# The output products of the mixing chain, issued in their own step

## The chip, the cores and the metric

The kernel runs on one core of a Trainium2 chip. The metric is device time in microseconds (us), as the median of several runs. Five engines matter here: TensorE (PE: matrix products, with PEld for its weight loads), VectorE (DVE), ScalarE (ACT), GpSimd (POOL) and SyncE (SP, which issues most transfers). Each engine works through its own list of instructions in order and waits on semaphores of the others.

## What is computed

A trunk of two layers over 768 tokens (256 context tokens, 512 latent tokens), width 1024. Each layer mixes tokens in three branches (convolution, differential attention, bidirectional RWKV-7), merges them and adds an MLP. The change is in the RWKV branch, whose core is a recurrence over time for each head and direction:

```
def step(s, inp):
    r_t, w_t, k_t, v_t, kk_t, a_t = inp
    sa = jnp.einsum('bhij,bhj->bhi', s, -kk_t)
    s = (s * w_t[:, :, None, :] + sa[..., None] * (kk_t * a_t)[:, :, None, :]
         + v_t[..., None] * k_t[:, :, None, :])
    return s, jnp.einsum('bhij,bhj->bhi', s, r_t)
```

It runs over 8 heads, forwards and backwards; the two directions' outputs are added.

## The kernel before

The recurrence is worked in chunks of 64 tokens. Two heads make a pair, there are four pairs in a layer, and both directions of a pair go along together. A pair has 12 chunks: two halves of three pieces (`gp` 0 to 5), a piece having two chunks (`q` 0 and 1). For a half, a triangular system is inverted ahead (`half_solve`: products `wps` and `jps`), and then `chain_piece` carries the state X from chunk to chunk. A chunk is a **step** of the chain, 48 in a layer and 96 in all, and has three visits to PE, each of which waits for the one before:

- first products, `ca<-x,ar`: the state against this chunk's rows; then DVE adds (`rhs`);
- second products, `ca<-rhs,j` and `cb<-rhs,j`: the inverse against `rhs`; then ACT and DVE write half of the result each into the tile `gv`;
- third products, `ca<-gv,tok`: the state's update; then DVE adds it to the decayed old state `xp` (made on ACT) and has the new X.

The chunk's outputs are two more kinds of products that are summed in one PSUM tile, `psy` (one buffer for a piece, tag "y", `bufs=1`): `psy<-tr,gv` (four products) and `psy<-ar,x` (four, with the state from before the update; none in a pair's first chunk, where the state is zero). Once a piece's two chunks are in, two instructions copy or add `psy` into the tile `y`: on ACT where `gp` is 0, 2 or 3, on DVE else. Layer 0 needs all outputs, layer 1 only those of latent tokens (`gp` 2 to 5).

Before the change, these products come one step late. A step leaves a note in `self.y_job`; the next step calls `y_products` (line 1264) right behind its own first products, so all eight stand there together, sorted by place, the two kinds in turn. `y_outs` (line 1286) puts the copies behind the next step's `gv` instructions. At the end of a half both are called once more.

PE also has the big products of the whole layer (`mmps`, line 228 like all products, in runs of 128x512 or 128x256), which are independent of the chain for long stretches. What stands in what order is set at build time: `weave` (line 283) keeps a clock for each engine by estimated costs, and takes at each point, of all streams of work (the chain is one, the big products another), the one whose next piece can start first. A stream says with `yield t, engine` when its next piece is ready. A fifth number in the yield, `STICK` (0.2 us), lets the chain go ahead although its input is that much short of ready. The second and third visits had it.

Of the kernel before, what the change touches and what calls it, by code (L numbers as in the profile page):

```python
# [10 lines left out]
F32 = mybir.dt.float32  # L11
F32R = mybir.dt.float32r
I32 = mybir.dt.int32
AF = mybir.ActivationFunctionType
ALU = mybir.AluOpType
# [4 lines left out]
P = 128  # L20
# [33 lines left out]
STICK = 0.2  # L54
# [66 lines left out]
class Trunk:  # L121
# [1139 lines left out]
                self.free("b1", t)  # L1261
        self.x_t = max(self.x_t, t)

    def y_products(self):

        if self.y_job is None:
            return
        st, pi, q, X, first, y = self.y_job
        self.y_job = None
        n, ar, tr, gv = st["n_half"], st["ar"], st["trs"][pi], st["gvs"][pi]  # L1270
        c = 2 * pi + q
        if q == 0:
            self.psy = self.rw.tile([P, 512], F32, tag="y", name="psy", bufs=1)[:, 0:256].rearrange("p (d c t) -> p d c t", d=2, c=2)
        for d in range(2):
            g = 1 - (q ^ d)
            for h in range(2):
                hc = slice(64 * h, 64 * h + 64)
                e = self.product(self.psy[hc, d, q, :], gv[:, 2 * d + q, hc], tr[:, q, g, h, :],
                                 start=True, stop=first, tile_position=(0, 64 * h))
                if not first:  # L1280
                    e = self.product(self.psy[hc, d, q, :], X[:, d, hc], ar[:, d, c, 1, :],
                                     start=False, stop=True, tile_position=(0, 64 * h))
        if q == 1:
            self.y_out = (st, pi, y, e)

    def y_outs(self):

        if self.y_out is None:
            return
        st, pi, y, e = self.y_out  # L1290
        self.y_out = None
        S, V = self.S, self.V
        gp = 3 * st["hh"] + pi
        psy = self.psy
        yield e, "ACT" if gp in (0, 2, 3) else "DVE"
        t0 = [x - self.c0 for x in (128 * gp, 128 * (1 - gp) if gp < 2 else 896 - 128 * gp)]
        for d in range(2):
            src = psy[:, d].rearrange("p c t -> p (c t)")
            if d == 1:
                src = src[:, ::-1]  # L1300
            dst = y[:, t0[d]:t0[d] + 128]
            if gp in (0, 2, 3):
                t = S.activation(out=dst, in_=src, func=AF.Copy)
            else:
                t = V.tensor_tensor(out=dst, in0=src, in1=dst, op=ALU.add)
        st["pp"]["y_t"] = t
        self.pieces[st["n_half"]] = pi

    def chain_piece(self, pi, st, y, need_y):
        pr, S, V = self.pr, self.S, self.V  # L1310
        hh, ar, pc = st["hh"], st["ar"], st["pc"]
        tok, gv, j, tv = st["toks"][pi], st["gvs"][pi], st["j"], st["tvs"][pi]
        gp = 3 * hh + pi
        self.x_t = max(self.x_t, st["tok_t"][pi])
        for q in range(2):
            c = 2 * pi + q
            first = gp == 0 and q == 0
            last = gp == 5 and q == 1
            X = self.xs[self.xi % 2]
            yield self.x_t, "PE"  # L1320
            ga = self.rw.tile([P, 512], F32, tag="ca", name="ca", bufs=1)
            gb = self.rw.tile([P, 512], F32, tag="cb", name="cb", bufs=1)
            gd = [1 - (q ^ d) for d in range(2)]
            gr = [slice(64 * g, 64 * g + 64) for g in gd]
            if first:
                rhs = tv[:, q, :]
            else:
                for d in range(2):
                    e = self.product(ga[gr[d], 0:128], ar[:, d, c, 0, :], X[:, d, :], start=True, stop=True,
                                     tile_position=(0, 64 * gd[d]))  # L1330
                self.y_products()
                if not last:
                    xp = pr.tile([P, 2, 128], F32, tag="xp", name="xp", bufs=1)
                    for d in range(2):
                        S.activation(out=xp[:, d, :], in_=X[:, d, :], func=AF.Copy, scale=pc[:, d, c:c + 1])
                yield e, "DVE"
                rhs = pr.tile([P, 128], F32, tag="rhs", name="rhs", bufs=1)
                t = V.tensor_tensor(out=rhs, in0=ga[:, 0:128], in1=tv[:, q, :], op=ALU.add)
                yield t, "PE", None, None, STICK
            gps = [ga[:, 256:384], gb[:, 0:128]]  # L1340
            for h in range(2):
                hc = slice(64 * h, 64 * h + 64)
                for d in range(2):
                    e = self.product(gps[d][gr[d], hc], j[gr[d], c, h, :], rhs[gr[d], hc], start=True, stop=True,
                                     tile_position=(64 * gd[d], 64 * gd[d]))
            yield e, "DVE"
            t = max(S.activation(out=gv[gr[0], q, :], in_=gps[0][gr[0], :], func=AF.Copy, scale=-1.0),
                    V.tensor_scalar(out=gv[gr[1], 2 + q, :], in0=gps[1][gr[1], :], scalar1=-1.0, scalar2=None, op0=ALU.mult))
            yield from self.y_outs()
            yield t, "PE", None, None, STICK  # L1350
            if not last:
                for d in range(2):
                    for h in range(2):
                        hc = slice(64 * h, 64 * h + 64)
                        e = self.product(ga[hc, 128 + 64 * d:192 + 64 * d], tok[:, d, q, hc], gv[:, 2 * d + q, hc],
                                         start=True, stop=True, tile_position=(0, 64 * h))
                yield e, "DVE"
                Xn = self.xs[(self.xi + 1) % 2]
                for h in range(2):
                    hc = slice(64 * h, 64 * h + 64)  # L1360
                    src = ga[hc, 128:256].rearrange("p (d t) -> p d t", d=2)
                    if first:
                        self.x_t = V.tensor_copy(out=Xn[hc, :, hc], in_=src)
                    else:
                        self.x_t = V.tensor_tensor(out=Xn[hc, :, hc], in0=src, in1=xp[hc, :, hc], op=ALU.add)
                self.xi += 1
            if need_y:
                self.y_job = (st, pi, q, X, first, y)
        if not need_y:
            self.pieces[st["n_half"]] = pi  # L1370
        elif pi == 2:
            yield t, "PE"
            self.y_products()
            yield from self.y_outs()

    def pair_bonus(self, l, p):
        V = self.V
# [100 lines left out]
    def chain(self, l, c0):  # L1478
        for n in range(8):
            p, hh = n // 2, n % 2  # L1480
            pp = self.pairs[p]
            yield 0.0, "DVE", lambda: self.halves[n] is not None and "j_t" in self.halves[n]
            st = self.halves[n]
            st["n_half"] = n
            yield st["j_t"], "DVE"
            yield from self.half_solve(st)
            self.solved = n
            for pi in range(3):
                yield 0.0, "PE", lambda: st.get("n", 0) > pi
                if hh == 0 and pi == 0:  # L1490
                    yield 0.0, "PE", lambda: p < 2 or "out" in self.pairs[p - 2]
                    pp["y"] = self.pe.tile([P, T - c0], F32, tag="y", name="y", bufs=2)
                yield from self.chain_piece(pi, st, pp["y"], 128 * (3 * hh + pi) >= c0)
            if hh == 1:
                self.later.append(lambda p=p: self.pair_out(l, p, c0))

# [31 lines left out]
    def inputs(self, l, full, lat):  # L1528
# [4 lines left out]
        self.halves, self.pieces, self.solved = [None] * 8, [-1] * 8, -1  # L1533
        self.ready, self.stage_t = {}, 0.0
        self.conv_n, self.x_t = 0, 0.0
        self.y_job = self.y_out = None
        self.n_upad = 2
        if len(lat) == 1:
            self.n_upad = 1
# [6 lines left out]
        first = deque({"w": lw, "k": k, "a": la, "r": r, "v": v, "g": lg}[x] for x in UNITS[l])  # L1546
# [697 lines left out]
```

## Time and profile before

| | |
|---|---|
| three runs | 2921.22, 2925.59, 2925.92 us; median 2925.59 |
| the profiled execution | 2913.63 us, of which the span of instructions is 2911.8 us |
| PE / PEld / DVE / ACT / POOL busy | 2768.5 / 2229.7 / 1961.5 / 1299.9 / 104.9 us |
| mean granted TensorE clock | 0.986 |
| the chain's stretch, layer 0 | from 166 to 560 us |
| the chain's stretch, layer 1 | from 1774 to 2213 us |

How to read it: PE is busy in 95% of the span, and the last chain of work runs over PE for 73%. A busy share hides two things, though. A product's row in the trace lasts longer than the distance to the next one, since products overlap, so a short wait can lie within a busy stretch; distances between starts tell more than durations. And each fp32 product of the chain has two rows (the first of the two kinds above: 320 products, 640 rows); the big products have one each.

### The profile page before, as it was taken

What the parts mean: (1) busy time and instruction counts of PE and PEld (TensorE: products, weight loads), DVE (VectorE), ACT (ScalarE), POOL (GpSimd) and SP (SyncE); (2) the same over time, 40 slices, a digit from 0 to 9 for tenths busy, and PEclk for the clock granted to TensorE, in tenths of its full rate; (3) what the DMA queues carried; (4) which work ended last, traced back from release to release, by engine and by line L of the source; (5) the groups of instructions that cost most, each with busy time, mean ns of one, the idle gap of its engine ahead of it and who ended that gap; (6) DMA issues with size and microseconds to landing.
All of it is one profiled execution on the core that took longest, in us unless ns stands there. A gap on an engine that the chain in (4) does not pass through costs nothing.

```text
span 2911.8 us, 56372 instructions
## 1 busy us (share of the span) xinstructions
PE 2768.5 (95%) x22423; PEld 2229.7 (77%) x22423; DVE 1961.5 (67%) x4311; ACT 1299.9 (45%) x2522; POOL 104.9 (4%) x181
## 2 busy tenths in 40 slices
PE   8999999999999999999999999999999888899998
PEld 6777777777788887888888777777777656788887
DVE  6778787489995548764333569889985667644445
ACT  4556655455544224231313356556554653433333
POOL 0000000011000000000000000000000100000000
PEclk9999999999999999999999999999999999999999
DMA  5232223354237633553112223223245535322223
GB/s 210 65 77 70 74 79 90 115 151 127 72 124 271 242 119 120 183 186 101 63 62 69 96 70 86 66 83 83 73 120 155 146 119 160 130 97 96 95 95 104
DMA packets 247751, 330.96 MB, mean 114 GB/s; under 512 B 118256, under 2 KB 124032, under 8 KB 247360
## 3 DMA queue, kind: packets, MB, share of 16 engines
q1 hardware_dynamic: 242160, 311.63, 33.6%
q0 software_dynamic: 3712, 14.17, 2.0%
q8 instruction: 176, 2.88, 0.4%
q10 hardware_dynamic: 1616, 1.56, 0.2%
q14 instruction: 87, 0.71, 0.1%
HBM read 266.32 MB, written 47.60 MB: 108 GB/s over the span
## 4 chain that ended last, share of the span: by engine, by line
PE 73%; DVE 14%; ACT 4%; DMA 3%; issue 2%; SPq 0%; DVEq 0%; POOL 0%; ACTq 0%; POOLq 0%
PE mmps L228 60%; PE ca L228 3%; DVE cacc L92 2%; DVE wl L92 2%; DVE ast L92 2%; PE tps L228 1%; ACT wh L92 1%; PE psy L228 1%; PE jps L228 1%; PE wps L228 1%; PE tvps L228 1%; DVE ap L92 1%; DVE x L92 1%; PE atps L240 1%; PE sps L228 1%
## 5 line engine op out<-in xcount | busy, mean ns | idle before, releaser
L228 PE MATMUL mmps<-hh,wh 128*128 128x512 f32 (+1 forms) x2344 | 850.0, 363 | 22.1 <-DVE k L92 5.7
L228 PE MATMUL mmps<-hh,wl 128*128 128x512 f32 (+1 forms) x2344 | 843.3, 360 | 6.0 <-DVE wl L92 5.9
L228 PE MATMUL mmps<-hl,wh 128*128 128x512 f32 (+1 forms) x2344 | 843.6, 360 | 4.3 <-DVE hl L92 4.1
L92 DVE TENSOR_TENSOR wl<-wr,wh 128x512 fp32r<-128x512 f32 x596 | 412.2, 692 | 473.9 <-ACT wh L92 460.1
L92 ACT ACTIVATE wh<-wr 128x512 fp32r<-128x512 f32 x596 | 375.2, 630 | 707.6 <-PE mmps L228 656.9
L228 PEld LDWEIGHTS mmps<-hh,wh 128*128 128x128 f32 x2344 | 446.9, 191 | 93.4 <-issue 18.1
L228 PEld LDWEIGHTS mmps<-hh,wl 128*128 128x128 f32 x2344 | 446.1, 190 | 77.1 <-DVE wl L92 12.8
L228 PEld LDWEIGHTS mmps<-hl,wh 128*128 128x128 f32 x2344 | 447.3, 191 | 67.5 <-DVE hl L92 7.4
L228 PE MATMUL mmps<-ffl,wh 128*128 128x512 f32 (+1 forms) x792 | 279.3, 353 | 0.0
L228 PE MATMUL mmps<-ffh,wh 128*128 128x512 f32 (+1 forms) x792 | 278.1, 351 | 0.0
L228 PE MATMUL mmps<-ffh,wl 128*128 128x512 f32 (+1 forms) x792 | 277.1, 350 | 0.0
L92 DVE SCALAR_TENSOR_TENSOR cacc<-upad,dww,cacc 128x783 f32<-128x783 f32 (+1 forms) x240 | 215.1, 896 | 4.3
L228 PEld LDWEIGHTS mmps<-ffh,wh 128*128 128x128 f32 x792 | 149.1, 188 | 22.7
L228 PEld LDWEIGHTS mmps<-ffh,wl 128*128 128x128 f32 x792 | 148.9, 188 | 21.5
L228 PEld LDWEIGHTS mmps<-ffl,wh 128*128 128x128 f32 x792 | 149.4, 189 | 20.8
L92 DVE SCALAR_TENSOR_TENSOR x<-mmps,mod,x 128x512 f32<-128x512 f32 (+1 forms) x126 | 80.1, 636 | 46.2 <-PE mmps L228 44.8
L92 POOL TENSOR_TENSOR bk<-bk,pc 128x384 f32<-128x384 f32 x64 | 57.4, 927 | 1200.0 <-PE tps L228 1138.5
L92 DVE SCALAR_TENSOR_TENSOR sq<-mmps,rl 128x512 f32<-128x512 f32 x96 | 56.9, 596 | 40.0 <-ACT rl L92 39.9
L92 ACT ACTIVATE stage<-mmps 128x512 f32<-128x512 f32 (+1 forms) x116 | 59.1, 510 | 51.7 <-PE mmps L228 48.7
L92 ACT ACT_TABLE_LOAD x62 | 79.5, 1283 | 4.2 <-PE mmps L228 2.1
L92 ACT ACTIVATE rl<-mmps 128x512 f32<-128x512 f32 x96 | 49.3, 514 | 67.9 <-PE mmps L228 67.9
L92 DVE TENSOR_REDUCE ast<-sps 128x1 f32<-128x768 f32 (+1 forms) x80 | 67.5, 844 | 17.3 <-PE sps L228 17.3
(317 smaller groups left out, 4377.1 us busy)
## 6 DMA issues: line engine op xcount, KB each, us to landing
wr<-in_w_dram SPq DMA_DIRECT2D x268, 256.0 KB, 2.5
wr<-in_win_dram SPq DMA_DIRECT2D x236, 256.0 KB, 2.7
modw<-in_modw_dram SPq DMA_DIRECT2D x80, 512.0 KB, 4.6
wr<-in_pw_dram SPq DMA_DIRECT2D x48, 256.0 KB, 2.9
wr<-in_wo_dram SPq DMA_DIRECT2D x44, 256.0 KB, 2.6
g<-stage SPq DMA_DIRECT2D x24, 384.0 KB, 3.2
gate<-g SPq DMA_DIRECT2D x24, 384.0 KB, 3.8
scb<-in_modw_dram SPq DMA_DIRECT2D x16, 512.0 KB, 6.5
```

The costliest lines, as they stand in the source:

```text
L92: f(**kw)
L228: self.nc.tensor.matmul(out, lhsT, rhs, **kw)
L240: self.nc.tensor.transpose(out, src, self.ident)
```

## The change

The functions `y_products` and `y_outs` go, with `self.y_job` and `self.y_out`. A local function `outputs` issues the products in their own step: the four `psy<-ar,x` right behind the step's first products, and the four `psy<-tr,gv` right behind the third products, which read the same `gv`. The copies of a piece stand at the piece's end, after its second state update. The chain's first visit gets `STICK` too. The note that a piece is done (`self.pieces`, on which other streams wait) moves into `chain`.

```diff
+        psy = []
+
+        def outputs(pairs, q, end):
+
+            clear = not psy
+            if clear:
+                psy.append(self.rw.tile([P, 512], F32, tag="y", name="psy", bufs=1)[:, 0:256].rearrange("p (d c t) -> p d c t", d=2, c=2))
+            for i, (w, x) in enumerate(pairs):
+                d, h = i // 2, i % 2
+                e = self.product(psy[0][64 * h:64 * h + 64, d, q, :], w, x, start=clear and d == 0, stop=end and q == 1 and d == 1, tile_position=(0, 64 * h))
+            return e
...
-            yield self.x_t, "PE"
+            yield self.x_t, "PE", None, None, STICK
...
-                self.y_products()
+                if need_y:
+                    outputs([(X[:, d, 64 * h:64 * h + 64], ar[:, d, c, 1, :]) for d in range(2) for h in range(2)], q, False)
...
-            yield from self.y_outs()
             yield t, "PE", None, None, STICK
...
+            if need_y:
+                ey = outputs([(gv[:, 2 * d + q, 64 * h:64 * h + 64], tr[:, q, gd[d], h, :]) for d in range(2) for h in range(2)], q, True)
+            if not last:
                 yield e, "DVE"
...
-            if need_y:
-                self.y_job = (st, pi, q, X, first, y)
-        if not need_y:
-            self.pieces[st["n_half"]] = pi
-        elif pi == 2:
-            yield t, "PE"
-            self.y_products()
-            yield from self.y_outs()
+        if need_y:
+            yield ey, "ACT" if gp in (0, 2, 3) else "DVE"
+            t0 = [x - self.c0 for x in (128 * gp, 128 * (1 - gp) if gp < 2 else 896 - 128 * gp)]
+            for d in range(2):
+                src = psy[0][:, d].rearrange("p c t -> p (c t)")
+                if d == 1:
+                    src = src[:, ::-1]
+                dst = y[:, t0[d]:t0[d] + 128]
+                if gp in (0, 2, 3):
+                    t = S.activation(out=dst, in_=src, func=AF.Copy)
+                else:
+                    t = V.tensor_tensor(out=dst, in0=src, in1=dst, op=ALU.add)
+            st["pp"]["y_t"] = t
...
                 yield from self.chain_piece(pi, st, pp["y"], 128 * (3 * hh + pi) >= c0)
+                self.pieces[n] = pi
```

On PE, near the end of layer 1's chain, this is the order before, from the last output products behind a step's first visit to the third visit and on (names as above; `hh`, `hl` and `wh`, `wl` are the high and low parts of inputs and weights):

```order
L228 MATMUL psy<-tr,gv 64x64
L228 MATMUL psy<-ar,x_18086 64x64
L228 MATMUL psy<-tr,gv 64x64
L228 MATMUL psy<-ar,x_18086 64x64
L228 MATMUL ca<-rhs,j 64x64
L228 MATMUL cb<-rhs,j 64x64
L228 MATMUL ca<-rhs,j 64x64
L228 MATMUL cb<-rhs,j 64x64
L228 MATMUL mmps<-hh_17325,wh 128x512
L228 MATMUL mmps<-hl_17326,wh 128x512
L228 MATMUL ca<-gv,tok 64x64 x4
L228 MATMUL mmps<-hh_17325,wl 128x512
```

Now, in the same place, from the first visit on:

```order
L228 MATMUL ca<-x_18086,ar 64x128 x2
L228 MATMUL psy<-ar,x_18086 64x64 x4
L228 MATMUL mmps<-hl_17326,wh 128x512
L228 MATMUL ca<-rhs,j 64x64
L228 MATMUL cb<-rhs,j 64x64
L228 MATMUL ca<-rhs,j 64x64
L228 MATMUL cb<-rhs,j 64x64
L228 MATMUL mmps<-hh_17325,wl 128x512
L228 MATMUL mmps<-hh_17311,wh 128x512
L228 MATMUL ca<-gv,tok 64x64 x4
L228 MATMUL psy<-tr,gv 64x64 x4
L228 MATMUL mmps<-hl_17312,wh 128x512
```

Half of the output products have moved from between the first and second visits to behind the third, and a big product stands between the first two visits.

On DVE, at the last change from one piece to the next in layer 1 (`x` is the new state, `rhs` the next step's sum, `y` the copies of the old piece), the order before:

```order
L92 TENSOR_TENSOR x_18087<-ca,xp 64x2x64 x2
L92 TENSOR_TENSOR rhs<-ca,tv 128x128
L92 TENSOR_SCALAR gv<-cb 64x128
L92 TENSOR_TENSOR y<-psy,y 128x128 x2
L92 TENSOR_TENSOR x_18086<-ca,xp 64x2x64 x2
```

And now:

```order
L92 TENSOR_TENSOR x_18087<-ca,xp 64x2x64 x2
L92 TENSOR_TENSOR y<-psy,y 128x128 x2
L92 TENSOR_TENSOR rhs<-ca,tv 128x128
L92 TENSOR_SCALAR gv<-cb 64x128
L92 TENSOR_TENSOR x_18086<-ca,xp 64x2x64 x2
```

The copies have moved ahead of the next step's `rhs`.

## Rows read from the trace of the kernel before

**Rows 1.** Busy time by stretch: window, length, PE, PEld, DVE, ACT, POOL, clock, DMA.

```profile
166.00:560.00 394.00, 381.53 (x5536) 299.05 (x5534) 288.55 (x861) 221.42 (x505) 22.53 (x36) 1.00 0.29 77
1774.00:2213.00 439.00, 423.30 (x5660) 315.03 (x5659) 381.23 (x1006) 239.08 (x524) 29.26 (x42) 1.00 0.31 84
```

**Rows 2.** PE's waits in layer 0's stretch: total us, times, longest.

```profile
PE wps L228 <- DVE jt L92: 3.5, 5, 1.3
PE ca L228 <- DVE rhs L92: 2.3, 7, 0.6
```

**Rows 3.** PE's waits in layer 1's stretch, same columns.

```profile
PE ca L228 <- DVE rhs L92: 2.1, 6, 0.6
PE ca L228 <- ACT gv L92: 1.4, 3, 0.7
```

**Rows 4.** Timeline, one step in layer 1: start us, duration us, engine, instruction.

```profile
2203.50 0.44 PE L228 MATMUL ca<-x,ar 128*64 128x128 f32 x4
...
2203.77 0.34 PE L228 MATMUL psy<-tr,gv 128*64 128x64 f32 x4
...
2203.99 0.29 DVE L92 TENSOR_TENSOR rhs<-ca,tv 128x128 f32<-128x128 f32 x1
...
2204.39 0.27 PE L228 MATMUL ca<-rhs,j 64*64 64x64 f32 x1
...
2204.77 0.50 PE L228 MATMUL mmps<-hh,wh 128*128 128x512 f32 x1
...
2205.10 0.40 PE L228 MATMUL mmps<-hl,wh 128*128 128x512 f32 x1
...
2205.43 0.45 PE L228 MATMUL ca<-gv,tok 128*64 128x64 f32 x8
...
2205.81 0.50 PE L228 MATMUL mmps<-hh,wl 128*128 128x512 f32 x1
...
2206.00 0.59 DVE L92 TENSOR_TENSOR x<-ca,xp 64x128 f32<-64x128 f32 x2 [0.79 <-PE ca L228]
2206.15 0.39 PE L228 MATMUL mmps<-hh,wh 128*128 128x512 f32 x1
...
2206.38 0.39 PE L228 MATMUL mmps<-hl,wh 128*128 128x512 f32 x1
...
2206.94 0.44 PE L228 MATMUL ca<-x,ar 128*64 128x128 f32 x4
```

**Rows 5.** Timeline of PE in layer 0, a step with four output products alone.

```profile
266.89 0.44 PE L228 MATMUL ca<-x,ar 128*64 128x128 f32 x4
267.16 0.40 PE L228 MATMUL psy<-tr,gv 128*64 128x64 f32 x8
267.49 0.39 PE L228 MATMUL mmps<-hl,wh 128*128 128x256 f32 x1
```

**Rows 6.** Timeline, the copies of a piece, on ACT and on DVE.

```profile
2201.73 0.45 ACT L92 ACTIVATE y<-psy 128x128 f32<-128x128 f32 x2
...
2208.56 0.47 DVE L92 TENSOR_TENSOR y<-psy,y 128x128 f32<-128x128 f32 x2
```

**Rows 7.** Timeline, the last solve of layer 0: products, copies, next products.

```profile
535.40 0.95 PE L228 MATMUL wps<-jt,ta 32*32 32x32 f32 x48
...
536.42 0.56 DVE L92 COPY jt<-wps 32x384 f32<-32x384 f32 x1 [1.36 <-PE wps L228]
...
537.41 0.95 PE L228 MATMUL jps<-j,jt 32*32 32x32 f32 x48
```

**Rows 8.** Tile view of psy: rows, duration min/median/max, first and last start.

```profile
L228 PE MATMUL psy<-tr,gv x640: 219/222/272, 170.3 to 2212.9; 128*64 128x64 f32 x160
L228 PE MATMUL psy<-ar,x x608: 221/222/223, 174.7 to 2213.0; 128*64 128x64 f32 x152
```

**Rows 9.** The page's groups: the loads of ACT's function tables, total and mean ns.

```profile
L92 ACT ACT_TABLE_LOAD x62 | 79.5, 1283 | 4.2 <-PE mmps L228 2.1
```

More of the change, by code (lines that the diff above doesn't have):

```diff
@@ L1262, in half_solve @@
         self.x_t = max(self.x_t, t)
[L1264 to L1306, printed above, removed]
-        self.pieces[st["n_half"]] = pi
     def chain_piece(self, pi, st, y, need_y):
@@ L1311, in chain_piece @@
         hh, ar, pc = st["hh"], st["ar"], st["pc"]
-        tok, gv, j, tv = st["toks"][pi], st["gvs"][pi], st["j"], st["tvs"][pi]
+        tr, tok, gv, j, tv = st["trs"][pi], st["toks"][pi], st["gvs"][pi], st["j"], st["tvs"][pi]
         gp = 3 * hh + pi
+        psy = []
[7 more added lines that the diff above has]
+            return e
         self.x_t = max(self.x_t, st["tok_t"][pi])
@@ L1366, in chain_piece @@
                 self.xi += 1
-            if need_y:
-                self.y_job = (st, pi, q, X, first, y)
-        if not need_y:
-            self.pieces[st["n_half"]] = pi
-        elif pi == 2:
-            yield t, "PE"
-            self.y_products()
-            yield from self.y_outs()
+        if need_y:
[11 more added lines that the diff above has]
+            st["pp"]["y_t"] = t
     def pair_bonus(self, l, p):
@@ L1483, in chain @@
             st = self.halves[n]
-            st["n_half"] = n
             yield st["j_t"], "DVE"
@@ L1535, in inputs @@
         self.conv_n, self.x_t = 0, 0.0
-        self.y_job = self.y_out = None
         self.n_upad = 2
```

## The prediction

> **What bounds the kernel now.** I read the busy time by stretch first. In the two stretches in which the chain runs PE is busy 381.5 of 394 us and 423.3 of 439 us, at full clock [rows 1]; DVE comes next with 381 of 439. So both stretches are as long as PE's work plus PE's waits, about 12.5 and 15.7 us of idle time. The view of waits says what they are: the solve's products waiting for a DVE copy, second visits waiting for `rhs` (2.3 and 2.1 us), third visits waiting for `gv` [rows 2, 3]. Then I read one step in the timeline, to see distances and not durations [rows 4].
>
> The order of both kernels says how far the change reaches. On PE the rows are the same up to the first solve of layer 0, again from the first transpose of the attention to the second layer's solve, and again from the second attention on; each time the attention begins at the same big product (the 1210th and the 6538th width of 512 in both). All products are the same in kind and number. So the big products are the filling of a stretch whose content is fixed: a chain that runs faster ends earlier among them (1139 instead of 1150 in layer 0; 6477 instead of 6472 in layer 1, so there later) and brings the end of the stretch no nearer. What can change is PE's cost of going from one kind of product to another, and its waits.
>
> **The change part by part.**
>
> *A, more alternation.* A big product follows another after 0.23 us (2206.15 to 2206.38). Two of them between the second and third visits take 0.66 us (2204.77 to 2205.43) [rows 4], so an entry of the big products among the small ones costs 0.66 - 0.46 = 0.20 us in all. Counted in the order, the runs of big products (with the normalizing sums) go from 619 to 638. Between first and second visits there are 26 more, since four output products fill half the time that eight did: 41 of 88 such places had only output products in them, none has now. Between third and next first visits there are 20 fewer; the rest are elsewhere. 19 x 0.20 = +3.8 us.
>
> *B, the output products beside their like.* Before: first visit with eight output products 0.27 + 0.62 (2203.50 to 2203.77 to 2204.39), third visit 0.38 (2205.43 to 2205.81) [rows 4]: 1.27 us. The step with four alone shows 0.27 + 0.33 [rows 5]; four behind the third visit, with the same shape, save the 0.10 us that a change of kind costs, so 0.38 - 0.10 + 0.33 = 0.61. After: 0.60 + 0.61 = 1.21. That is -0.06 us; as the 0.62 holds a few hundredths of waiting that belong to C, I take -0.05 for 76 steps (608 rows of `psy<-ar,x`, eight a step [rows 8]) and the same for 16 ends of halves, which had a visit of eight by itself: -4.6 us.
>
> *C, waits for `rhs`.* The first visit starts at 2203.50, `rhs` is done on DVE at 2204.28, the second visit starts at 2204.39: 0.89 us are needed, and first visit and eight products fill just that [rows 4]. With four products and one big one they fill 0.27 + 0.33 + 0.43 = 1.03 (0.43 being 0.23 + 0.20). Of the 4.4 us of idle time before second visits [rows 2, 3] some come from a DVE that is busy elsewhere, and stay: I take half, -2.2 (0 to -4.4).
>
> *D, waits for the new state.* From the third visit to DVE's end of the new state is 2206.59 - 2205.43 = 1.16 us, and with the 0.10 us that `rhs` needed to reach PE, 1.26 [rows 4]. I added up, with distances as above, what the order puts between the third visit and the next first: before, one place of 88 is short of 1.26; now 18 are, as the chain may start 0.2 us early there, by 2.2 us together. +2.2 (0 to +4.4: 18 places at 0.2 us and a margin).
>
> *E, the one buffer for outputs.* A new wait. The next piece's first output products now come one visit after the last piece's; they wait for its copies, and behind them on PE everything waits. The order has 24 such waits, 12 on DVE and 12 on ACT. DVE: copies follow the new state at once and take 0.47 us [rows 6]; the first visit starts 0.10 to 0.35 us after the new state (2206.59 to 2206.94) and its output products 0.27 later, so they stand 0 to 0.2 us. The next `rhs` stands behind the copies on DVE, but starts 0.49 us after the first visit anyway. ACT: the copies can start when the last `psy` product is through, some 0.8 us after the third visit, and take 0.45 [rows 6], so they are done at 1.25, before 1.53 (1.26 + 0.27), unless ACT has something else ahead; in the order it has (an exponential, a split, a copy) in 3 of 12. So 12 x 0.08 + 3 x 0.2 = +1.5, 0.08 and 0.2 being my choice within 0 to 0.2 and 0 to 0.45. The bounds: 0, and 24 full copies, 24 x 0.47 = 11.
>
> *F, the solves and token tiles.* The fills around them change as the mixture moves. Products, copy and next products take 2.0 us from start to start (535.40 to 537.41) [rows 7]; in the new order one solve of layer 0 has only 0.88 us between, and four other places are 0.1 to 0.25 short. +2.0 (-4 to +4: the solves' waits of 3.5 us in layer 0 [rows 2] as the size of what such places move).
>
> *G, ACT.* The order has six more table loads (63 to 69), at 1.28 us [rows 9]: 7.7 us on an engine busy 221 of 394 us [rows 1]. Hidden by its idle time; a few hold back a `gv`. +0.5 (0 to 7.7).
>
> Sum: 3.8 - 4.6 - 2.2 + 2.2 + 1.5 + 2.0 + 0.5 = +3.2 us. On the profiled execution that is 2913.6 + 3.2 = 2916.8; the median of the runs stands 12 us above that execution, and 2925.6 + 3.2 gives **2929**. The runs before differ by 4.7 us, and 0.2% (5.9 us) is about what a measurement of this kernel can tell from no change.
>
> **The rivals.**
>
> *The buffer decides (slower).* Place: the 24 waits of E. Point: copies that end later than 0.27 us after the first visit's start. For it: DVE in layer 1 is 87% busy [rows 1], ACT's queue has whole conversions and table loads of 1.28 us [rows 9], and the planner, which knows nothing of this wait, will not have put anything before it. Against: the chain's rows come first on both engines. At a full copy, +11 instead of +1.5, it gives 2938; slower.
>
> *The drain decides.* The rows show that a product of one kind behind one of another costs about 0.1 us more: 0.33 for four products of which the last is followed by a big one [rows 5], 0.20 for an entry and an exit [rows 4]. If only such changes of kind cost, and the sorting of eight output products into four and four saves nothing, B is zero and the sum 3.2 + 4.6 = +7.8: 2933; slower by 0.27%. For it: the 0.05 us of B are a small difference of rows from two places, one in each layer. Against: the first visits in the two places agree, 0.27 us each [rows 4, 5]. The Trainium skill, TensorEngine Tiling (Array Packing), section Key Properties, says that changing the tiling mode drains TensorE, while changing the tile alone does not. By that rule this rival is right: output products and third products have one mode, and putting them together removes no change of mode. The trace agrees on the cost of an entry (0.20 us) but has no row of the two side by side.
>
> *The waits go (faster).* The chain gets its own way more often (the early start for the first visit, fewer big products between): C in full, -4.4, and none of D to G, as a chain that is ahead has its inputs ready: 3.8 - 4.6 - 4.4 = -5.2, and with the waits for `gv` (1.4 us [rows 3]) and half of the solve's 3.5 [rows 2] gone -8.3: 2917 to 2920. For it: in layer 0 the chain ends 11 widths of big products earlier. Against: in layer 1, where `gv` was waited for, it ends 5 later.
>
> *Nothing moves.* All terms lie within 5 us, and could cancel; this is the forecast's own middle and has no case of its own.
>
> **How the numbers follow.** Forecast (2923 to 2933, mostly within 0.2%) 0.47; the buffer 0.22; the drain 0.12; the waits go 0.19. Faster by over 0.2%: most of the last, and a little for an order that falls well, 0.17. Slower by over 0.2%: buffer and most of the drain, and the upper edge of the forecast, 0.35. Same: 0.48. The range reaches from 2916 (the waits go, in full) to 2940 (the buffer at a full copy and two more), and leaves out what lies beyond both: a solve or an attention that starts late for a reason that the order doesn't show.
>
> **What would show it.** The stretches grow by some 2 us each at the same number of products. B: a third visit and its four output products take 0.61 us from first start to the next kind. C: waits for `rhs` fall to about half of 4.4 us. D: waits for the new state come up, near 2 us. E: a group of waits of `psy` for `y`, on DVE up to 0.2 us each; if they are near 0.5, the buffer decides. A: two big products between visits still take 0.66. The prediction is wrong if the attention no longer starts at the same big product, if the time after 560 and 2213 us changes by more than the runs do, or if one wait of several us appears that no step here names.

## The result, and the profile after

The changed kernel takes 2938.9 us (median of six runs, 2929.2 to 2943.9), the kernel before 2921.5 in the same count of runs: a ratio of 1.0055, 95% interval 1.0034 to 1.0075. It is slower by 17 us, or 0.6%.

The profiled execution of the changed kernel took 2943.9 us, that of the kernel before 2913.6: the first is the slowest of its runs, the second faster than any of the six timed runs before, so the two traces differ by 30 us where the medians differ by 17. I come back to the other 13. First the stretches that answer to [rows 1], same columns; the third number from the end is the granted clock as a share of 2.4 GHz.

```profile
166.00:565.00 399.00, 384.33 (x5534) 297.35 (x5528) 292.19 (x866) 228.92 (x511) 21.40 (x36) 1.00 0.28 74
1786.00:2239.00 453.00, 432.54 (x5664) 322.07 (x5662) 382.09 (x1005) 239.47 (x525) 29.91 (x42) 0.97 0.30 84
```

The stretches are longer by 5 and 14 us; in the second the clock is 0.97 where it was full. For a fair comparison of all kernels I cut the span into five stages that hold the same work everywhere: up to layer 0's first solve; from there to the 2210th big product (width of 512); to layer 1's first solve; to the 7400th big product; the rest. Busy time by stage of the kernel before, second and fourth stage:

```profile
155.40:896.70 741.30, 706.85 (x7561) 564.56 (x7561) 588.00 (x1356) 409.35 (x860) 41.44 (x72) 0.99 0.34 100
...
1780.00:2533.20 753.20, 697.48 (x6871) 522.98 (x6871) 586.24 (x1381) 397.69 (x813) 43.88 (x75) 0.98 0.39 114
```

and all five of the changed kernel:

```profile
0.00:156.30 156.30, 144.30 (x1025) 111.01 (x1025) 106.60 (x309) 78.09 (x147) 11.05 (x23) 0.96 0.42 135
156.30:904.90 748.60, 711.57 (x7561) 563.96 (x7561) 590.37 (x1356) 417.09 (x866) 40.31 (x72) 0.99 0.34 99
904.90:1791.50 886.60, 861.82 (x5298) 736.40 (x5297) 501.50 (x947) 285.16 (x479) 8.58 (x12) 0.99 0.38 128
1791.50:2563.10 771.60, 710.02 (x6871) 531.15 (x6871) 587.48 (x1380) 397.65 (x813) 44.75 (x75) 0.96 0.38 111
2563.10:2941.70 378.60, 363.50 (x1675) 299.64 (x1673) 179.79 (x322) 129.94 (x224) 0.00 (x0) 0.98 0.29 96
```

Stage two grew by 7.3 us, stage four by 18.4. The other three hold the same work in the same order and differ by 0.9, 3.3 and 0.0. PE's waits in the two stretches come next. Before, the groups that stand beside [rows 2, 3] (layer 0, then layer 1):

```profile
PE ca L228 <- DVE x L92: 0.4, 1, 0.4
```

```profile
PE wps L228 <- DVE jt L92: 2.5, 4, 1.0
...
PE jps L228 <- DVE jt L92: 1.9, 5, 0.7
...
PE ca L228 <- DVE x L92: 0.5, 2, 0.4
```

After the change, the groups that answer to them and those that grew (layer 0, then layer 1):

```profile
PE wps L228 <- DVE jt L92: 4.3, 7, 1.4
...
PE ca L228 <- DVE x L92: 1.4, 4, 0.5
...
PE ca L228 <- DVE rhs L92: 0.2, 1, 0.2
```

```profile
PE wps L228 <- DVE jt L92: 5.1, 7, 1.3
PE ca L228 <- DVE rhs L92: 3.6, 8, 1.4
PE jps L228 <- DVE jt L92: 2.2, 7, 0.4
PE ca L228 <- DVE x L92: 2.1, 5, 0.9
```

Waits for `rhs` left layer 0 and came back in layer 1. Waits for the new state (`x`), 0.9 us in three places before, are 3.5 us in nine. The solves wait longest. One ordinary step in the timeline, to set beside [rows 4]:

```profile
2228.25 0.45 PE L228 MATMUL ca<-gv,tok 128*64 128x64 f32 x8
2228.53 0.40 PE L228 MATMUL psy<-tr,gv 128*64 128x64 f32 x8
2228.82 0.59 DVE L92 TENSOR_TENSOR x<-ca,xp 64x128 f32<-64x128 f32 x2 [0.81 <-PE ca L228]
2228.86 0.50 PE L228 MATMUL mmps<-hh,wl 128*128 128x512 f32 x1
2229.20 0.40 PE L228 MATMUL mmps<-hh,wh 128*128 128x512 f32 x1
2229.56 0.44 PE L228 MATMUL ca<-x,ar 128*64 128x128 f32 x4
2229.80 0.43 PE L228 MATMUL psy<-ar,x 128*64 128x64 f32 x8
2230.16 0.50 PE L228 MATMUL mmps<-hl,wh 128*128 128x512 f32 x1
```

Third visit and output products take 0.61 us (2228.25 to 2228.86), first visit and output products 0.60 (2229.56 to 2230.16), both as worked out. From the third visit to the next first visit it is 1.31 us, all of it the way through DVE: the state is written by 2229.41 and PE starts 0.15 later. The last big product started at 2229.20 and gave way after 0.36 us where 0.33 is usual; no row calls that a wait. A big product is recorded as 0.40 long although the next one starts 0.23 after it, so a wait shorter than that difference stands in no list. I therefore also compare start to start: what a run of products of one kind took ahead of a first visit, less what the same run takes at places where nothing is waited for. By that measure the time lost ahead of first visits went from 1.8 to 9.0 us. The size hangs on the pace that is called usual: with the shortest case of the same run in the same trace it goes from 3.6 to 8.0. The Trainium skill, Perfetto Trace Analysis, section Tensor Engine Instruction (MATMUL, LD_WEIGHTS), says that TensorE's reported end is computed from the size of the instruction and not observed; the 0.40 beside a pace of 0.23 fits that.

The longest listed wait for the state is of another kind:

```profile
1898.65 0.45 PE L228 MATMUL ca<-gv,tok 128*64 128x64 f32 x8
...
1899.36 0.53 DVE L92 COPY x<-ca 64x128 f32<-64x128 f32 x2
...
1900.03 0.44 PE L228 MATMUL ca<-x,ar 128*64 128x128 f32 x4 [0.93 <-DVE x L92]
```

DVE is hardly late here: the state is written 1.24 us after the third visit's start, where the ordinary step above takes 1.16. But layer 1 has no output products in this piece, the order has no big product there either, and so PE stands for most of the way through DVE. At other places DVE does come late:

```profile
1981.58 0.45 PE L228 MATMUL ca<-gv,tok 128*64 128x64 f32 x8
...
1982.16 0.56 DVE L92 SCALAR_TENSOR_TENSOR e<-e,e 128x384 f32<-128x384 f32 x1
...
1982.75 0.59 DVE L92 TENSOR_TENSOR x<-ca,xp 64x128 f32<-64x128 f32 x2
...
1983.48 0.44 PE L228 MATMUL ca<-x,ar 128*64 128x128 f32 x4 [0.38 <-DVE x L92]
```

DVE, in the middle of another stream's work, has the state written 1.76 us after the third visit, 0.6 us later than in the ordinary step. What stands between third and first visit covers only a part of that.

### The profile page after: what moved, and what is told of

Its sections match the earlier page's. It is cut to its first block, busy times and chain, and to the rows that moved or that the text cites. A ratio compares the mean times of both kernels' runs of the same rounds, so it can differ in the third digit from the quotient of the medians.

```text
span 2941.7 us, 56384 instructions
## 1 busy us (share of the span) xinstructions
PE 2791.2 (95%) x22423; PEld 2242.2 (76%) x22423; DVE 1965.7 (67%) x4311; ACT 1307.9 (44%) x2528; POOL 104.7 (4%) x181
## 5 line engine op out<-in xcount | busy, mean ns | idle before, releaser
L228 PE MATMUL mmps<-hh,wh 128*128 128x512 f32 (+1 forms) x2344 | 854.9, 365 | 18.8 <-ACT wh L92 5.8
L92 DVE TENSOR_REDUCE ast<-sps 128x1 f32<-128x768 f32 (+1 forms) x80 | 67.5, 844 | 18.3 <-PE sps L228 18.3
```

The source lines that it names most:

```text
L92: f(**kw)
L228: self.nc.tensor.matmul(out, lhsT, rhs, **kw)
```

## The experiments

My theory after the traces was that the early start of first visits and the solves make the 17 us; the rivals were the one buffer and the fall of the order alone. All kernels ran beside the kernel before (2921.7, 2922.8 and 2923.1 us in the three groups of four). This table has what the traces of all of them say; "at the limit" counts the first visits, of 88, that start within 1.32 us of the third visit; "lost" is the time ahead of first visits, start to start; "solves" is PE's listed idle time before the solves' products; the stages are two and four, in us.

| kernel | median (runs) | ratio and interval | stage 2 | stage 4 | at the limit | lost | solves |
|---|---|---|---|---|---|---|---|
| before | 2921.5 (6) | | 741 | 753 | 1 | 1.8 | 12.1 |
| sorted_alone | 2919.1 (12) | 0.9991 [0.9977, 1.0006] | 742 | 754 | 1 | 1.8 | 12.3 |
| second_order_before | 2922.3 (12) | 0.9998 [0.9989, 1.0006] | 747 | 755 | 1 | 2.5 | 13.4 |
| other_order_before | 2930.7 (8) | 1.0027 [1.0015, 1.0039] | 746 | 763 | 2 | 2.2 | 16.5 |
| margin_before | 2925.9 (12) | 1.0013 [1.0003, 1.0023] | 740 | 778 | 0 | 3.2 | 5.6 |
| early_first_alone | 2932.6 (8) | 1.0039 [1.0024, 1.0054] | 751 | 757 | 37 | 7.9 | 19.7 |
| late_first | 2932.6 (9) | 1.0036 [1.0022, 1.0050] | 750 | 757 | 9 | 2.1 | 18.3 |
| other_order_late | 2941.9 (6) | 1.0066 [1.0052, 1.0079] | 752 | 765 | 20 | 3.3 | 18.8 |
| late_margin | 2931.8 (12) | 1.0028 [1.0016, 1.0040] | 741 | 767 | 12 | 4.0 | 4.5 |
| after | 2938.9 (6) | 1.0055 [1.0034, 1.0075] | 749 | 772 | 34 | 9.0 | 17.6 |
| two_halves | 2937.7 (6) | 1.0049 [1.0032, 1.0066] | 748 | 760 | 34 | 8.1 | 17.1 |
| second_order_after | 2928.3 (12) | 1.0018 [1.0007, 1.0030] | 754 | 760 | 31 | 7.2 | 15.7 |
| other_order_after | 2953.9 (4) | 1.0103 [1.0087, 1.0120] | 762 | 761 | 34 | 8.1 | 17.2 |
| margin_after | 2934.4 (8) | 1.0035 [1.0021, 1.0050] | 742 | 771 | 36 | 8.8 | 7.9 |

A stage's length in one trace holds its clock too: 0.95 in stage four of margin_before, 0.96 and 0.97 in those of after, margin_after, late_first and late_margin, 0.98 in the rest.

### The early start, taken out and put in alone

late_first is the changed kernel with

```diff
-            yield self.x_t, "PE", None, None, STICK
+            yield self.x_t, "PE"
```

and early_first_alone the kernel before with the same line turned the other way.

> The changed kernel without the early start of first visits (the planner's head start of 0.2 us stays on second and third visits, as in the kernel before). Theory 1, the early first visit makes the waits: PE then waits less for the new state and the chain's planned times match again, so 2921 to 2927, within 0.2% of the kernel before. Theory 2, the one buffer for the outputs: the copies are as late as they were, so no change against the changed kernel, 2935 to 2942. Theory 3, where the solves fall among the DVE's other work: the fill is dealt anew, so any value from 2920 to 2940, and the sum of PE's waits for the solve's copies (9.5 us in layer 1's chain and 9.3 in layer 0's after the change, 6 and 5 before) moves with it.

> The kernel before with the one part alone: first visits may start 0.2 us before the new state is due. Theory 1: most of the 17 us are there, 2932 to 2940. Theory 2: nothing of them, 2919 to 2925. Theory 3: the order is dealt anew, 2918 to 2935, with the size in the waits around the solves and not in the waits for the new state. The order has 41 places with less than 1.305 us between a third visit and the next first, by 2.6 us in all, so the waits for the new state alone are worth about 2.6 us.

Without it the changed kernel takes 2932.6 us, 6 less than with it, but 11 more than the kernel before. Alone it costs the kernel before 11 us. Neither part gives the 17, and the two alone (11 and 11) come to more than both together. Theory 1 had asked for 2921 to 2927 without the early start, which missed, and for 2932 to 2940 with it alone, which holds; the wide ranges of theory 3 hold both. In all, four pairs of kernels in the table differ in the early start and in what the planner makes of it. It costs 11 us on the kernel before, 12 on other_order_late, 6 on late_first and 3 on late_margin (which gives margin_after); the last two are not clear of the noise. The waits for the new state follow the early start alone. In layer 1, with it (early_first_alone):

```profile
PE wps L228 <- DVE jt L92: 5.4, 6, 1.9
PE ca L228 <- DVE x L92: 2.7, 8, 1.0
```

and without it (late_first):

```profile
PE wps L228 <- DVE jt L92: 3.8, 5, 1.9
...
PE ca L228 <- DVE x L92: 0.4, 2, 0.2
```

The table says the same of all kernels: with the early start 31 to 37 first visits at the limit and 7.2 to 9.0 us lost, in six kernels; without it 0 to 20 and 1.8 to 4.0, in eight. The worst place of early_first_alone is one where DVE is busy with something else and has the state written 2.19 us after the third visit:

```profile
1862.45 0.45 PE L228 MATMUL ca<-gv,tok 128*64 128x64 f32 x8
...
1863.49 0.54 DVE L92 TENSOR_TENSOR t<-k,t 128x384 f32<-128x384 f32 x1
1864.05 0.59 DVE L92 TENSOR_TENSOR x<-ca,xp 64x128 f32<-64x128 f32 x2
...
1864.79 0.44 PE L228 MATMUL ca<-x,ar 128*64 128x128 f32 x4 [0.99 <-DVE x L92]
```

So this part is shown: by the start-to-start measure, 5 to 7 us of waits for the state in each of the four pairs. But early_first_alone also has 7.6 us more before its solves, and its 11 us are not the state's waits alone.

### The buffer, taken away

```diff
-                psy.append(self.rw.tile([P, 512], F32, tag="y", name="psy", bufs=1)[:, 0:256].rearrange(...
+                psy.append(self.psy[:, 256 * (gp % 2):256 * (gp % 2) + 256].rearrange(...
```

(`self.psy` is one tile for a layer's whole chain; successive pieces use its two halves.)

> The changed kernel with the outputs of successive pieces in alternating halves of the bank, so that no product waits for the copies of the piece before; the order of all engines stays as it is. Theory 2, the buffer: 2925 to 2930, at least 8 us off the changed kernel. Theories 1 and 3: at most the 1.5 us of the forecast's term E, so 2936 to 2939, not to be told from the changed kernel.

2937.7 against 2938.9 (ratios of 1.0049 and 1.0055): no difference that can be measured, and not the 2925 to 2930 that theory 2 asked for. Start to start, the time ahead of output products went from 2.4 to 1.2 us. The buffer is worth about 1 us, and does not decide.

### The output products sorted

```diff
-                e = self.product(self.psy[hc, d, q, :], gv[:, 2 * d + q, hc], tr[:, q, g, h, :],
-                                 start=True, stop=first, tile_position=(0, 64 * h))
-                if not first:
-                    e = self.product(self.psy[hc, d, q, :], X[:, d, hc], ar[:, d, c, 1, :],
-                                     start=False, stop=True, tile_position=(0, 64 * h))
...
+            prods = [(X[:, d, 64 * h:64 * h + 64], ar[:, d, c, 1, :], d, h) for d in range(2) for h in range(2)] + prods
+        for i, (wt, x, d, h) in enumerate(prods):
+            e = self.product(self.psy[64 * h:64 * h + 64, d, q, :], wt, x, start=q == 0 and i < 2,
+                             stop=q == 1 and i >= len(prods) - 2, tile_position=(0, 64 * h))
```

With the sequence, the marks for where a sum starts and stops (`start`, `stop`) change too: before, each output's first product starts a sum; here only the first two products of a piece do, as in the changed kernel.

> The kernel before with the eight output products of a visit sorted: four with the state, then four with gv, instead of taking turns; every order stays as it is. If products beside their like are cheaper (term B) the eight take 0.57 and not 0.62 us, 92 times: -4.6 us, so 2917. If only a change to or from big products costs (the drain decides), 2921 to 2922, no change.

The time, 2919.1, is 2.7 us below its group's 2921.7, with an interval that holds both answers. The timeline decides, beside the first rows of [rows 4]:

```profile
2203.20 0.44 PE L228 MATMUL ca<-x,ar 128*64 128x128 f32 x4
2203.47 0.40 PE L228 MATMUL psy<-ar,x 128*64 128x64 f32 x8
2203.70 0.40 PE L228 MATMUL psy<-tr,gv 128*64 128x64 f32 x8
2204.04 0.27 PE L228 MATMUL ca<-rhs,j 64*64 64x64 f32 x1
```

From the first visit to the next kind it is 0.84 us; before, 0.89. At the 14 places where a big product of 128x512 follows directly it is 0.833 against 0.883 in the median. The eight products are 0.05 us cheaper, in up to 92 places, or 4.6 us of PE's time; whether by their sequence or by the marks, this run doesn't tell. What of it reaches the end is 2.7 us by the medians, between a gain of 6.7 and a loss of 1.8 by the interval; a part is given back, as PE comes to the second visits sooner than `rhs` does (listed waits 4.4 before, 5.4 here).

### The solves held back

margin_after is the changed kernel, margin_before the kernel before, with this line at both products of a solve (`wps` and `jps`):

```diff
-            yield t, "PE", None, lock
+            yield t + 0.7, "PE", None, lock
```

> The changed kernel in which the planner holds the solves' products on PE back by 0.7 us, behind each copy that they need; nothing else. Theory A, the solves' waits are what the chip pays for: in the changed kernel PE stands 9.5 us (wps and jps behind jt, both chains) where the copy on DVE comes up to 1.4 us late behind another stream's instruction; with big products put there instead, two thirds of that go, 2930 to 2934. Theory B, the waits only show where DVE is the bound, and come back at the next place that DVE feeds (rhs, the new state): 2935 to 2940, with more idle time before second visits.

> The kernel before with the same 0.7 us for the solves' products. Its solves wait 7.9 us in the profile (wps and jps behind jt, both chains). Theory A: two thirds of it go, 2916 to 2918. Theory B: no change, 2920 to 2924. If this one gains as much as the changed kernel does with it, the margin is a gain of its own and the solves are not what the change lost by.

The solves' idle time falls, from 17.6 to 7.9 and from 12.1 to 5.6 us. The changed kernel takes 2934.4, 4 us less, at the edge of what theory A expected. The kernel before takes 2925.9, 3 us more, against both theories. A part of both results goes with the clock. The 73 runs of the kernel before that stand beside the experiments have a mean granted clock of 0.983, margin_after and margin_before 0.981, and over the 73 runs each 0.001 goes with 1.9 us. Brought to 0.983 at that rate, an estimate, the medians are 2922 (kernel before), 2937 (changed), 2928.5 (margin_after) and 2922.6 (margin_before). So at one clock the changed kernel gains 8 us and the kernel before nothing, which by the test in the expectation above makes the solves' waits a part of what the change lost. Whether the lower clock is itself a price of these orders is not shown.

PE's listed waits in layer 0's chain fall from 13.2 to 7.0 us in margin_after, while layer 1's stay (18.5 and 18.3): there they have moved on.


```profile
PE jps L228 <- issue: 3.4, 4, 1.3
PE ca L228 <- DVE rhs L92: 3.4, 5, 1.6
...
PE wps L228 <- DVE jt L92: 0.7, 2, 0.4
```

Layer 0 keeps the gain: stage two is 742 us, as in the kernel before. Holding the solves back gives layer 0 its 7 us back, here and in late_margin below; in layer 1 other waits take their place.

### The order alone

The planner takes streams that are closer than `EPS` as level. other_order_before, other_order_after and other_order_late (on late_first) have 0.03, the two second orders 0.01:

```diff
-EPS = 0.02
+EPS = 0.03
```

> The kernel before with another tie break in the planner: streams closer than 0.03 us count as level, where it was 0.02. It does nothing by itself, and deals the fill around the chain anew (PE enters the big products 417 times in the two stretches, 414 before; one solve has 1.1 us too little between its products). Theory C, the fall of the order alone is worth 10 us and more, so that the 15 us need no cause in the change: any value from 2910 to 2940. Theory D, the change itself lost them: 2918 to 2927, one short solve being worth about 1 us.

> The changed kernel with the same other tie break. Theory C: any value from 2920 to 2945, no closer to the changed kernel than to the kernel before. Theory D: 2934 to 2941, and the waits for the new state stay near 9 us over the pace of products (25 us of all waits).

> The kernel before with the tie break at 0.01 us instead of 0.02: a third order of the same kernel. At one level of the mean granted clock (0.983) the first stands at 2922, the second at 2927. If the kernel before is a lucky order, 2925 to 2932; if its placement is what makes it fast, 2919 to 2925. Waits for the new state stay near 2 us over the pace in either case.

> The changed kernel with the tie break at 0.01 us: a third order of the changed kernel; the other two stand at 2937 and 2946 at a mean granted clock of 0.983. If the change has a price of its own whatever the order, 2933 or more, and the waits for the new state are again 8 to 9 us over the pace; if only the order decides, it may come out anywhere from 2922 to 2946.

> The changed kernel without the early start and with the tie break at 0.03 us: a second order of late_first, which stands at 2928 at a mean granted clock of 0.983. Without the early start the waits for the new state stay near 2 us over the pace. If the placement of the outputs alone costs nothing, it may come out at 2922 to 2928; if it costs some 6 us of its own, 2927 to 2934. The order has one solve with 0.6 us and another with 1.4 us too little between its products, 2.6 us in all, against 2.1 in late_first.

A tie break that means nothing moves the kernel before between 2922 and 2931 and the changed kernel between 2928 and 2954. Under each of the three tie breaks (0.01, 0.02, 0.03) the changed kernel is the slower one, by 6 (just clear of the noise), 17 and 23 us, and late_first by 11 under both of its two. What late_first loses its 11 us by is not shown; its solves wait longer, 18.3 us against 12.1. So the change has a price of its own in every order that was tried, and the size that was measured, 17, is as much a matter of the order: theory D holds for the sign, theory C for the size. Several of the expected ranges failed: other_order_before is above theory D's 2927, other_order_after and other_order_late are above both of theirs, and second_order_after, at 2928, is below the 2933 that a price in every order asked for. second_order_before, at 2922, is where its placement was to have it. Three orders are few, and a fourth in which the sign turns can't be excluded.

### Both parts out

```diff
-            yield self.x_t, "PE", None, None, STICK
+            yield self.x_t, "PE"
...
-            yield t, "PE", None, lock
+            yield t + 0.7, "PE", None, lock
```

> The changed kernel without the early start of first visits and with the solves' products held back by 0.7 us. In late_first the waits for the new state were 2.1 us over the products' pace (9.1 in the changed kernel) and those of the solves 14.4. If the two are the 15 us that the change costs at one level of the mean granted clock, both go here: 2919 to 2925, level with the kernel before. If the order's fall decides (each new order costs a few us somewhere), 2926 to 2934, with the waits at other places.

2931.8, where the two causes together should have given 2919 to 2925 at one level of the mean clock. This kernel's mean clock is 0.980; brought to 0.983 as above, its median is 2926, 4 us above the kernel before, where the changed kernel is 15 above. So at one clock the two parts take some 11 of the 15 us with them. Layer 0 is back at 741 us, layer 1 is not (767, at a clock of 0.97 against 0.98). That the waits for the state and the solves' waits are all of it is not shown: the 4 us have no cause here, nor has the lower clock. No kernel here beats the kernel before by more than the measurement tells; sorted_alone and second_order_before are the only ones below it, by 3 and by 1 us.

## Why the prediction was right or wrong

The time lies in the range of 2916 to 2940, at its very end; the forecast of 2929 is 10 us too low and "within 0.2%", which had the highest chance, is wrong: slower by over 0.2% had 0.35. The miss is larger than these 10 us: the forecast was +3.2 us on a kernel before of 2925.6, and the change is worth 17 on one of 2921.5. That the range holds the time is luck, as its upper end was set by the buffer at a full copy, which two_halves refutes. What bounds the kernel was read rightly: the attention begins at the same big products, and the time is PE's work plus PE's waits.

*A* (+3.8): the price of an entry holds: two big products between second and third visits still take 0.66 us (2227.59 to 2228.25). No run had more alternation and nothing else, so the sum was not tested.

*B* (-4.6): right in size on PE: the changed kernel's visits take 0.60 + 0.61 = 1.21 us, as forecast, and sorted_alone saves 0.05 us a visit; how much of it reaches the time is not measured closely enough. With it the drain rival falls, whose point was that sorting saves nothing, as far as it was the sorting and not the marks that saved it. The rule of the Trainium skill that was named there (TensorEngine Tiling (Array Packing), Key Properties: changing the mode drains TensorE, changing the tile does not) is not contradicted: the 0.05 us in eight products were saved within one mode. Whether by the kind of operand, by the tile that comes next or by the marks, the runs don't tell.

*C* (-2.2): too large. Listed waits for `rhs` went from 4.4 to 3.8 us: layer 0's went (2.3 to 0.2), layer 1's rose (2.1 to 3.6), where DVE is the busier engine.

*D* (+2.2, at most +4.4): the first step that failed. Measured 6 to 7 us (1.8 to 8.1 and 9.0 lost), or 4 at the shortest pace. Two things were off. The distance that is needed is 1.305 us and not 1.26, so 34 places are at the limit and not 18. And each was priced at its shortfall in the order, a tenth or two; in two_halves, nine places of more than 0.25 us hold 4.6 of the 8.1 us. In most of them DVE comes late, and a distance that holds exactly what is needed passes that lateness on to PE. Before, three quarters of the distances were 1.47 us and more; now a quarter are 1.31 at most.

*E* (+1.5): right, about 1. The rival "the buffer decides" named 2938, within a microsecond of the result, and is refuted by two_halves: a time that fits is no evidence for a cause.

*F* (+2.0, -4 to +4): the second step that failed. The solves' idle time went up by 5.5 us. I read the short places between products and copies from the order, but most of these waits (34 listed ones after, 25 before) are for an instruction on DVE that comes late, behind another stream's or behind a transfer, and PE's order shows neither. The longest of layer 0 after the change is one for a transfer, in which DVE itself stands for 1.95 us:

```profile
483.19 0.98 DVE L92 STREAM_TRANSPOSE jt<-j 128x768 f32<-128x768 f32 x1 [1.95 <-DMA j<-bout]
...
484.22 1.02 PE L228 MATMUL wps<-jt,ta 32*32 32x32 f32 x96 [1.36 <-DVE jt L92]
```

*G* (+0.5): six more table loads came, as counted:

```profile
L92 ACT ACT_TABLE_LOAD x68 | 87.2, 1283 | 3.2 <-PE mmps L228 2.1
```

and waits for `gv` went from 1.6 to 1.0 us, so they cost nothing that shows.

With the measured sizes of C to G and the forecast's A and B the sum is 3.8 - 4.6 - 0.6 + 6.8 + 1.0 + 5.5 = 11.9 of the 17 us, or 9.5 with the smaller size of D. What the rest is, is open. Open as well is how much of F belongs to the change: other_order_before has 16.5 us before its solves with no change at all. The list of what would prove the prediction wrong asked for a wait of several us or a changed time outside the chain; neither came. It should have asked for many small ones of a kind that was named.

## What to carry to other kernels

Where a planner deals out the work, an edit has two effects: its own, and a new order. Time a few orders that a meaningless constant deals out before believing a difference of half a per cent. And letting the critical chain start as early as its inputs can possibly be there takes away the margin that absorbed another engine's lateness: price such a place by how late that engine may be, not by the shortfall in the plan.

## What was not expected of the hardware

The clock falls, or doesn't, in the same order. The changed kernel and two_halves have the same order on every engine. In both, PE idles in pieces around a solve at 1946 to 1956 us. Busy time and clock (third number from the end) in 2.5 us windows, the changed kernel:

```profile
1953.50:1956.00 2.50, 1.78 (x62) 1.58 (x62) 2.47 (x6) 0.48 (x1) 0.00 (x0) 1.00 0.00 0
1956.00:1958.50 2.50, 2.50 (x59) 2.15 (x57) 1.47 (x3) 0.63 (x1) 0.00 (x0) 0.58 0.02 7
1958.50:1961.00 2.50, 2.50 (x6) 1.62 (x6) 1.52 (x3) 1.06 (x3) 0.00 (x0) 0.50 0.01 3
```

and two_halves:

```profile
1953.50:1956.00 2.50, 1.80 (x62) 1.58 (x63) 2.47 (x6) 0.48 (x1) 0.00 (x0) 1.00 0.00 0
1956.00:1958.50 2.50, 2.50 (x62) 2.17 (x61) 1.50 (x4) 1.38 (x4) 0.00 (x0) 1.00 0.03 7
```

The one drops to 1.2 GHz (0.50) until 1970 us, the other stays at 2.4. The changed kernel drops a second time, at 2031 us. Its stage four is 771.6 us, that of two_halves 759.9 at 0.98: of the 13 us that the two first traces differ beyond the medians, that is 11.7, about 1 of it the buffer's. The same happens ahead of the chain, where all is alike: 156.3 us at 0.96 in the changed kernel, in two_halves

```profile
0.00:161.00 161.00, 149.50 (x1027) 114.11 (x1027) 106.98 (x309) 78.40 (x147) 11.03 (x23) 0.92 0.40 132
```

Over the 73 runs of the kernel before (2914 to 2938 us) each 0.001 of the mean granted clock goes with 1.9 us, so the mean clock, which every run lists, should be read beside a time. The Trainium skill, TensorE: Matmul & The Clock Gate, section What's actually happening, says that the gate looks at the engine's activity on a cycle of its own, so that one kernel measures differently from run to run; these two traces agree.
